# Three of the four weight sums of a seven-product matmul moved from VectorE to accumulating DMAs

## The chip, the core and the metric

The kernel runs on one core of one Trainium2 chip. The metric is the device time of one execution in microseconds (us). The kernel before takes 1199.08 us in the median of three runs (1198.47 to 1199.55).

## The reference, cut to what matters

The program is one layer of a decoder trunk for 512 tokens of width 1024, all in float32. What the change touches is the first mixer, retention with four heads. For each head h the layer projects the normed input u onto q and k (256 columns each), v (512 columns) and a gate g (512 columns), and then retains:

```
u = rmsnorm(h, g_pre_mix)
rq, rk, rv, rg, ... = split(u @ w_in)
yr = retention(rq, rk, rv, positions)          # scores, decay, scores @ v, chunk by chunk
yr = rmsnorm(yr) * silu(rg)
ya_branch = yr @ w_ret_out
```

Behind it come the dilated attention's output, two merge gates, `w_o`, an MLP with a squared ReLU (`w_up`, `w_down`), and a last gated projection. None of that is touched.

## The kernel before

**Splitting.** A float32 product is made of three TensorE passes in the fp32r type. Each operand is split into a high part (ScalarE writes the rounded copy, line 66) and a low part (VectorE subtracts it from the source, line 69): `split`, lines 71 to 73. The passes are high*high, high*low and low*high.

**Weight units.** Weights come in units of 256 rows by 512 columns, 512 KB, a raw tile of 128 partitions by 1024 elements. SyncE loads them in the order of the list `loads` (`load_next`, line 94). The list `plan` says how the raw tile of each unit is come by. `prep_next` (line 121) takes the next plan entry, makes a `w` tile of six in a ring and splits into it. It is called each time TensorE's program has used up one unit (line 744), so units are prepared some five ahead, and a split waits until the unit six back has been used.

**Seven products.** A head's v and g columns together are one matmul of 512 tokens by 1024 by 1024. It is done as a 2x2 block product with seven block products in place of eight. The order (`EARLY`, line 139) is 11, 1, 12, 2, 4, 7, 22; each product takes two weight units, k=0 and k=1. The weight blocks are quarters of `w_in`, written here by their indices: (0,0), (0,1), (1,0), (1,1). Four of the seven products need sums of quarters, per unit k:

- product 11 takes x = (0,0) as it is;
- product 1 takes x + y with y = (0,1);
- product 12 takes (1,0) as it is;
- product 2 takes x + y + z with z = (1,1);
- product 4 takes z as it is;
- product 7 takes y + z;
- product 22 takes x + y + z + (1,0), and (1,0) is loaded a second time for it.

The sums are made in place by VectorE (`add`, line 149, through `tt`, line 69): the rows `t<-t,t 128x1024`. So a head has 4 sums times 2 units, 8 of them, and 10 unit loads.

**A head on TensorE.** `head` (line 772) runs the q and k projection (line 256), the products 11 and 1 (line 740), the scores (line 812), the products 12, 2, 4 and 7, the retention of the first two token blocks (line 827), the product 22 and the retention of the other two. Products 11 and 12 share a pair of PSUM banks, 1 and 4 another, and 2, 7 and 22 a third. The scores go to banks of the same pool as the third pair, which has four: product 2 can begin only after VectorE has multiplied scores with the decay (`s<-b,dec`) and freed banks. The result of product 1 (`s<-a,s`, line 707) must be read before product 4 adds to its banks.

**GpSimd.** In this stretch it does one thing, the power -0.5 for each retained token block (`rstd`, line 327, operation `st<-st,mhalf`). VectorE's gate multiply (line 833) waits for it, and TensorE later transposes the gate's result (line 849).

**The order of instructions** on each engine is set by a scheduler when the program is built. The order on TensorE is the program's; on the others it goes by priorities and the scheduler's own clock.

Of the kernel before, what the change touches and what calls it, by code (L numbers as in the profile page):

```python
# [14 lines left out]
OP = mybir.AluOpType  # L15
# [16 lines left out]
def hybrid_block(ctx, tc, a, out):  # L32
    nc = tc.nc
# [16 lines left out]
    def big(shape=(P, D), dtype=F32):  # L50
        return pt.tile(list(shape), dtype, name=nm("t"), tag="t")
# [13 lines left out]
    def act(o, i, f=AF.Copy, **kw):  # L65
        nc.scalar.activation(o, i, f, **kw)  # L66

    def tt(o, x, y, op):
        nc.vector.tensor_tensor(o, x, y, op=op)  # L69

    def split(hi, lo, src):
        act(hi, src)
        tt(lo, src, hi.bitcast(F32), OP.subtract)
# [16 lines left out]
    loads, plan = [], []  # L90
    raws, ready = [], []
    ptr = {"dma": 0, "prep": 0}

    def load_next():
        if ptr["dma"] < len(loads):
            r = big((P, 2, 512))
            load(r, loads[ptr["dma"]])
            raws.append(r)
            ptr["dma"] += 1

    def pop():
        if not raws:
            load_next()
        return raws.pop(0)

    def new_w():
        return pw.tile([P, 2, 2, 512], F32R, name=nm("w"), tag="w")
# [3 lines left out]
    def divide(w, r, gain):  # L111
        if gain is None:
            split(w[:, 0], w[:, 1], r)
            return
        n, k0 = gain
        for k in range(2):
            g = cols[:, n, k0 + k:k0 + k + 1]
            act(w[:, 0, k], r[:, k], AF.Copy, scale=g)
            stt(w[:, 1, k], r[:, k], g, w[:, 0, k].bitcast(F32), OP.mult, OP.subtract)

    def prep_next():
        if ptr["prep"] == len(plan):
            return
        ptr["prep"] += 1
        r = plan[ptr["prep"] - 1]()
        w = new_w()
        divide(w, r, row_gain.get(ptr["prep"] - 1))
        ready.append(w)
        while len(raws) < N_RAW - 1 and ptr["dma"] < len(loads):
            load_next()  # L130

    def add_units(w, n, gain=None):
        for kk in range(w.shape[1]):
            loads.append(w[n, kk])
            if gain is not None:
                row_gain[len(plan)] = (gain, 2 * kk)
            plan.append(pop)

    EARLY, LATE = ("11", 1, "12", 2, 4, 7, "22"), ("11", 1, 2, 4, 7, "12", "22")

    def add_quartet(quarter, order, between=(), nk=2, gaps=(1, 1, 1, 1, 1, 1, 2)):
        x, y, z, v = {}, {}, {}, {}
        again = order is EARLY

        def keep(d, k):
            d[k] = pop()
            return d[k]

        def add(a, b):
            tt(a, a, b, OP.add)  # L150
            return a

        make = {
            "11": ((0, 0), lambda k: keep(x, k)),
            1: ((0, 1), lambda k: add(x[k], keep(y, k))),
            2: ((1, 1), lambda k: add(x[k], keep(z, k))),
            4: (None, lambda k: z[k]),
            7: (None, lambda k: add(y[k], z[k])),
            "12": ((1, 0), lambda k: pop() if again else keep(v, k)),
            "22": ((1, 0) if again else None, lambda k: add(x[k], pop() if again else v[k])),  # L160
        }
        for name in order:
            src, f = make[name]
            for k in range(nk):
                if src is not None:
                    loads.append(quarter(*src, k))
                plan.append(lambda f=f, k=k: f(k))
            m = gaps[order.index(name)]
            for src, f, gain in between[:m]:
                loads.append(src)  # L170
                row_gain[len(plan)] = gain
                plan.append(f)
            between = between[m:]

    w_in, w_ro, w_do = a["w_in"], a["w_ret_out"], a["w_dil_out"]
# [5 lines left out]
    for h in range(H):  # L181
        add_units(w_in, 3 * h)
        if not h:
            for n in range(2):
                add_units(w_do, n)
        add_quartet(lambda kh, nh, k, h=h: w_in[3 * h + 2 - nh, 2 * kh + k], EARLY)
    for h in range(H):
        for n in range(2):
            add_units(w_ro[h], n)
# [13 lines left out]
    for c in range(NC):  # L203
        ups = [(a["w_up"][2 * c + 2 + j, k], pop, (3, 2 * k)) for j in range(2 if c + 1 < NC else 1) for k in range(4)]
        add_quartet(lambda kh, nh, k, c=c: a["w_down"][2 * c + kh, nh, k], EARLY, ups, 2, gaps_of(c))
    ups = [(a["w_up"][NFC - 1, k], pop, (3, 2 * k)) for k in range(4)]
    add_quartet(lambda kh, nh, k: a["w_down"][NFC - 2, nh, kh], EARLY, ups, 1, SOME)
    for n in range(2):
        add_units(a["w_down"][NFC - 1], n)
# [51 lines left out]
    def gemm(nu, xT, evac, wstat=False, k_outer=False):  # L261
        us = take(nu)
        if k_outer:
            banks = [abank() for _ in range(4)]
            for k in range(2 * nu):
                for t in range(4):
                    acc_tile(banks[t], us, xT, t, wstat, None, [k])
                    if k == 2 * nu - 1:
                        if t == 3:
                            prep_next()  # L270
                        evac(t, banks[t])
                if k % 2 and k < 2 * nu - 1:
                    prep_next()
            return
        for t in range(4):
            ps = abank()
            acc_tile(ps, us, xT, t, wstat, prep_next if t == 3 else None)
            evac(t, ps)
# [14 lines left out]
    for i in range(4):  # L293
        x = big((P, 2, 512))
        r = big((P, 2, 512))
# [19 lines left out]
    def stt(o, x, s, y, op0=OP.mult, op1=OP.mult):  # L315
        return nc.vector.scalar_tensor_tensor(o, x, s, y, op0=op0, op1=op1)  # L316

    def rstd(parts, n, out=None):
        s = parts[0]
        for p2 in parts[1:]:  # L320
            s2 = stat()
            tt(s2, s, p2, OP.add)
            s = s2
        v = stat()
        nc.vector.tensor_scalar(v, s, 1.0 / n, EPS, op0=OP.mult, op1=OP.add)
        r = stat() if out is None else out
        nc.gpsimd.tensor_tensor(r, v, mhalf[:, :1], op=OP.pow)
        return r
# [21 lines left out]
    for i in range(4):  # L350
        w = new_w()
        r = pop()
        for j in range(2):
            f = 2 * i + j
            g = cols[:, 0, f:f + 1]
# [4 lines left out]
        ptr["prep"] += 1  # L360
        load_next()
    prep_next()
    uT = feed(u)

    rs0 = const.tile([P, NT], F32, name="rs0")
    for t in range(NT):
        x = xr[t]
# [564 lines left out]
    for t in range(NT):  # L932
        x = big()
# [82 lines left out]
    def part(t, n):  # L1016
        return facc[t][:, halves[n]]
# [66 lines left out]
    f = fs[0][0]  # L1084
# [11 lines left out]
    for t in range(NT):  # L1096
        parts = []
        for n in range(2):
# [4 lines left out]
            f = part(t, n)  # L1103
# [3 lines left out]
        with tc.high_priority():  # L1107
            r = rstd(parts, D)
# [34 lines left out]
    for t in range(NT):  # L1143
# [8 lines left out]
        with tc.high_priority():  # L1152
            r = rstd(parts[t], D)
# [80 lines left out]
```

## Time and profile before

| | before |
|---|---|
| median of three runs | 1199.08 us |
| the profiled execution | 1198.07 us |
| its span, first to last instruction | 1196.3 us |
| TensorE busy | 1183.7 us (99%) |
| VectorE busy | 813.7 us (68%) |
| ScalarE busy | 588.5 us (49%) |
| GpSimd busy | 65.3 us (5%) |
| moved by DMA | 158.35 MB |

The span begins with the first instruction and ends with the last; the profiled execution's own time holds 1.8 us more around it. Busy is the time in which an engine had an instruction running. The profile calls TensorE PE (its weight loads PEld), VectorE DVE, ScalarE ACT, GpSimd POOL and SyncE SP. L69 is line 69 of the kernel; many operations are issued by a helper and share its line, so the tile names tell them apart: `w` is a split weight unit, `t` a raw or other big tile, `s` a half tile, `a` and `b` PSUM banks, `dec` the decay.

### The profile page before, as it was taken

How to read it: one execution, taken by the hardware profiler on the slowest of the kernel's cores; microseconds unless marked ns; L12 is line 12 of the kernel's file. 1: busy time of each engine (PE TensorE's matmuls, PEld its weight loads, DVE VectorE, ACT ScalarE, POOL GpSimd, SP SyncE). 2: the span in 40 equal slices, each digit the busy share in tenths (PEclk: the TensorE clock that was granted, in tenths of full speed). 3: DMA queues.
4: the chain of work that ended last, by engine and by line, in shares of the span. 5: the costliest groups of instructions: out<-in, count | busy, mean ns of one | idle time of the engine just before them, and what ended most of it. 6: DMA issues, size and time to landing. Idle time of an engine off the chain costs nothing.

```text
span 1196.3 us, 15173 instructions
## 1 busy us (share of the span) xinstructions
PE 1183.7 (99%) x5634; PEld 985.7 (82%) x5634; DVE 813.7 (68%) x1243; ACT 588.5 (49%) x1031; POOL 65.3 (5%) x112
## 2 busy tenths in 40 slices
PE   9999999999999999999999999999999999999996
PEld 7888888888888888888888888888888888888885
DVE  6753653664748995959678457663575775988885
ACT  7335524537545553535445622365553654544562
POOL 1002101000000010010100020020000000000210
PEclk9999999999999999999999999999999999999999
DMA  9431141432422542442336563735241251335401
GB/s 345 152 111 58 59 154 36 132 122 95 158 98 80 202 158 98 133 153 89 110 106 211 171 216 111 269 110 233 71 160 59 98 193 36 111 134 207 171 13 71
DMA packets 53178, 158.35 MB, mean 132 GB/s; under 512 B 8816, under 2 KB 9072, under 8 KB 53104
## 3 DMA queue, kind: packets, MB, share of 16 engines
q1 hardware_dynamic: 39408, 131.29, 31.7%
q10 hardware_dynamic: 9600, 14.54, 3.7%
q0 software_dynamic: 4096, 11.55, 2.7%
q8 instruction: 44, 0.72, 0.3%
q14 instruction: 30, 0.25, 0.1%
HBM read 138.96 MB, written 14.68 MB: 128 GB/s over the span
## 4 chain that ended last, share of the span: by engine, by line
PE 97%; ACT 1%; DVE 1%; DMA 1%; SPq 0%; issue 0%; ACTq 0%; DVEq 0%; POOLq 0%
PE a L256 53%; PE b L740 17%; PE a L1063 11%; PE a L740 7%; PE b L827 2%; PE b L531 2%; PE b L812 1%; PE b L495 1%; PE b L520 1%; ACT t L66 1%; PE b L339 1%; PE b L849 1%; DMA t<-in_w_in_dram 1%; DVE t L316 0%; DVE t L504 0%; PE b L623 0%
## 5 line engine op out<-in xcount | busy, mean ns | idle before, releaser
L256 PE MATMUL a<-u,w 128*128 128x512 f32 x1536 | 358.7, 392 | 1.2 <-ACT t L66 0.7
L256 PEld LDWEIGHTS a<-u,w 128*128 128x128 f32 x1536 | 285.7, 188 | 61.5 <-issue 1.0
L66 ACT ACTIVATE w<-t 128x1024 fp32r<-128x1024 f32 (+1 forms) x211 | 217.7, 1042 | 209.4 <-PE a L256 71.6
L69 DVE TENSOR_TENSOR w<-t,w 128x1024 fp32r<-128x1024 f32 (+1 forms) x211 | 251.4, 1200 | 95.1 <-ACT w L66 93.4
L69 DVE TENSOR_TENSOR t<-t,t 128x1024 f32<-128x1024 f32 (+4 forms) x193 | 196.6, 1043 | 32.5 <-ACT t L66 18.1
L740 PE MATMUL b<-w,t 128*128 128x512 f32 x780 | 182.7, 390 | 0.0
L740 PEld LDWEIGHTS b<-w,t 128*128 128x128 f32 x780 | 146.1, 188 | 31.2 <-ACT t L66 0.7
L1063 PE MATMUL a<-u,w 128*128 128x512 f32 x576 | 134.8, 389 | 0.0
L1063 PEld LDWEIGHTS a<-u,w 128*128 128x128 f32 x576 | 108.1, 188 | 22.5
L256 PE MATMUL a<-w,u 128*128 128x512 f32 (+1 forms) x504 | 113.2, 383 | 0.2 <-DVE w L69 0.2
L256 PE MATMUL a<-t,w 128*128 128x512 f32 x480 | 109.7, 390 | 0.0
L256 PEld LDWEIGHTS a<-w,u 128*128 128x128 f32 x504 | 91.3, 189 | 18.8 <-DVE w L69 0.5
L256 PEld LDWEIGHTS a<-t,w 128*128 128x128 f32 x480 | 89.9, 188 | 18.6
L316 DVE SCALAR_TENSOR_TENSOR w<-t,cols,w 128x512 fp32r<-128x512 f32 x80 | 57.5, 747 | 45.4 <-ACT w L66 45.3
L69 DVE TENSOR_TENSOR t<-a,t 128x512 f32<-128x512 f32 x64 | 50.3, 788 | 48.0 <-ACT t L66 34.3
L256 PE MATMUL a<-w,t 128*128 128x512 f32 x336 | 78.3, 392 | 0.0
L256 PEld LDWEIGHTS a<-w,t 128*128 128x128 f32 x336 | 62.4, 188 | 13.2 <-DVE t L69 0.3
L66 ACT ACTIVATE w<-t,cols 128x512 fp32r<-128x512 f32 x80 | 53.9, 716 | 38.4 <-PE a L1063 27.2
L66 ACT ACTIVATE t<-t 128x512 fp32r<-128x512 f32 (+1 forms) x62 | 46.3, 768 | 29.6 <-DVE t L69 28.7
L66 ACT ACTIVATE t<-s 128x256 f32<-128x256 f32 (+3 forms) x98 | 42.3, 476 | 26.5 <-DVE s L69 25.6
L69 DVE TENSOR_TENSOR s<-a,t 128x512 f32<-128x512 f32 x40 | 26.0, 686 | 41.3 <-PE a L256 30.7
L66 ACT ACTIVATE t<-t,st 128x128 f32<-128x128 f32 (+1 forms) x96 | 39.7, 416 | 26.8 <-DVE st L507 26.8
(120 smaller groups left out, 1028.8 us busy)
## 6 DMA issues: line engine op xcount, KB each, us to landing
t<-in_w_in_dram SPq DMA_DIRECT2D x104, 512.0 KB
t<-in_w_down_dram SPq DMA_DIRECT2D x39, 512.0 KB
t<-in_w_up_dram SPq DMA_DIRECT2D x32, 512.0 KB
t<-in_w_ret_out_dram SPq DMA_DIRECT2D x16, 512.0 KB
t<-in_x_dram SPq DMA_DIRECT2D x8, 512.0 KB
yrd<-s ACTq DMA_DIRECT2D x16, 256.0 KB
t<-yrd SPq DMA_DIRECT2D x16, 256.0 KB
t<-in_w_o_dram SPq DMA_DIRECT2D x8, 512.0 KB
```

Source lines behind the costliest of these rows:

```text
L66: nc.scalar.activation(o, i, f, **kw)
L69: nc.vector.tensor_tensor(o, x, y, op=op)
L256: nc.tensor.matmul(ps, l, r, start=(k == 0 and q == 0), stop=(k == n - 1 and q == 2))
L316: return nc.vector.scalar_tensor_tensor(o, x, s, y, op0=op0, op1=op1)
L339: nc.tensor.transpose(b[:, f * P:(f + 1) * P], src[:, f * P:(f + 1) * P], ident)
L495: nc.tensor.matmul(sb[hh][:, q * w:(q + 1) * w], at(qT, p0 + q)[rows, t * P:(t + 1) * P], at(kT, p0 + q)[rows, k0:k0 + w], start=True, sto ...
L520: nc.tensor.transpose(tb[:, c * P - h0:(c + 1) * P - h0], sm[:, i, j * P:(j + 1) * P], ident)
L531: nc.tensor.matmul(pv[:, s * HD:(s + 1) * HD], got["t"][:, c * P:(c + 1) * P], at(v, t - nb + 1 + j)[:, s * HD:(s + 1) * HD], start=(j == ...
L740: nc.tensor.matmul(ps[t], f(k, i, t), w[:, j, k2], start=(first and k == 0 and n == 0), stop=(k == 2 * nk - 1 and n == 2), skip_group_chec ...
L812: nc.tensor.matmul(b[:, :w], kT[d][:, i1, j * P:(j + 1) * P], qT[d][:, i2, j * P:], start=(n == 0), stop=(n == 5))
L827: nc.tensor.matmul(b, sc[j][:, i1, c:c + P], vh[j][:, i2, :], start=(n == 0), stop=(n == last))
L1063: nc.tensor.matmul(state["ps"][t], w[:, i, k2, t * P:(t + 1) * P], vT[:, x, k], start=(k == 0 and n == 0), stop=(k == 7 and n == 2))
```

## The change

In the heads' seven-product form (and not in the MLP's) the sums for the products 2, 7 and 22 are no longer made by VectorE. `add_quartet` gets a flag, set in the heads. With it, a DMA issued by GpSimd reads a quarter from DRAM and adds it onto the raw tile where that lies (`pour`, with `accum_op=OP.add`). After the split of product 1's unit k, two such DMAs add (1,1) onto x and onto y; after the split of product 2's unit k, one adds (1,0) onto x. Products 2, 7 and 22 then split x and y as they find them. Product 4's (1,1) becomes a load of its own, the loads for 2 and 22 go. The first sum, x + y for product 1, stays with VectorE.

```diff
--- before.py
+++ after.py
@@ -122,9 +122,13 @@
         if ptr["prep"] == len(plan):
             return
         ptr["prep"] += 1
-        r = plan[ptr["prep"] - 1]()
+        f = plan[ptr["prep"] - 1]
+        f, g = f if isinstance(f, tuple) else (f, None)
+        r = f()
         w = new_w()
         divide(w, r, row_gain.get(ptr["prep"] - 1))
+        if g:
+            g()
         ready.append(w)
         while len(raws) < N_RAW - 1 and ptr["dma"] < len(loads):
             load_next()
@@ -138,7 +142,7 @@
 
     EARLY, LATE = ("11", 1, "12", 2, 4, 7, "22"), ("11", 1, 2, 4, 7, "12", "22")
 
-    def add_quartet(quarter, order, between=(), nk=2, gaps=(1, 1, 1, 1, 1, 1, 2)):
+    def add_quartet(quarter, order, between=(), nk=2, gaps=(1, 1, 1, 1, 1, 1, 2), by_dma=False):
         x, y, z, v = {}, {}, {}, {}
         again = order is EARLY
 
@@ -159,12 +163,26 @@
             "12": ((1, 0), lambda k: pop() if again else keep(v, k)),
             "22": ((1, 0) if again else None, lambda k: add(x[k], pop() if again else v[k])),
         }
+
+        def pour(d, k, src):
+            nc.gpsimd.dma_start(d[k], quarter(*src, k), accum_op=OP.add)
+
+        behind = {}
+        if by_dma:
+            make.update({
+                2: (None, lambda k: x[k]),
+                4: ((1, 1), lambda k: pop()),
+                7: (None, lambda k: y[k]),
+                "12": ((1, 0), lambda k: pop()),
+                "22": (None, lambda k: x[k]),
+            })
+            behind = {1: lambda k: (pour(x, k, (1, 1)), pour(y, k, (1, 1))), 2: lambda k: pour(x, k, (1, 0))}
         for name in order:
             src, f = make[name]
             for k in range(nk):
                 if src is not None:
                     loads.append(quarter(*src, k))
-                plan.append(lambda f=f, k=k: f(k))
+                plan.append((lambda f=f, k=k: f(k), behind.get(name) and (lambda g=behind[name], k=k: g(k))))
             m = gaps[order.index(name)]
             for src, f, gain in between[:m]:
                 loads.append(src)
@@ -183,7 +201,7 @@
         if not h:
             for n in range(2):
                 add_units(w_do, n)
-        add_quartet(lambda kh, nh, k, h=h: w_in[3 * h + 2 - nh, 2 * kh + k], EARLY)
+        add_quartet(lambda kh, nh, k, h=h: w_in[3 * h + 2 - nh, 2 * kh + k], EARLY, by_dma=True)
     for h in range(H):
         for n in range(2):
             add_units(w_ro[h], n)
```

Per head there are 6 accumulating DMAs of 512 KB, 8 loads in place of 10, and 2 sums on VectorE in place of 8; over four heads that is 24 DMAs more, 8 loads fewer and 24 VectorE instructions fewer. The order on TensorE is the same row for row.

On VectorE, in the third head (h = 2), before the change. `t612` and `t614` are x for k=0 and k=1, `t628` is y for k=0, `t665` and `t667` are z; `w678` and `w684` are the split units of product 2, `w686` that of product 4; `s687` and `s688` are the results of product 1; `s690` is the first score times decay:

```order
615 L69 TENSOR_TENSOR w678_4527<-t612_4176,w678_4527 128x1024
616 L69 TENSOR_TENSOR t614_4193<-t614_4193,t667_4477 128x1024
617 L69 TENSOR_TENSOR s687_4571<-a682_4536,s680_4532 128x512
618 L69 TENSOR_TENSOR t628_4245<-t628_4245,t665_4466 128x1024
619 L69 TENSOR_TENSOR s688_4573<-a683_4537,s681_4534 128x512
620 L69 TENSOR_TENSOR w684_4551<-t614_4193,w684_4551 128x1024
621 L69 TENSOR_TENSOR w686_4568<-t665_4466,w686_4568 128x1024
622 L69 TENSOR_TENSOR s690_4582<-b689_4575,dec534_3727 128x512
```

After the change, the same place. `t608` and `t610` are x for k=0 and k=1, `w674` and `w679` product 2's units, `w680` and `w696` product 4's, `s682` and `s683` the results of product 1, `s685` the first score times decay:

```order
602 L69 TENSOR_TENSOR w674_4522<-t608_4168,w674_4522 128x1024
603 L69 TENSOR_TENSOR w679_4544<-t610_4185,w679_4544 128x1024
604 L69 TENSOR_TENSOR w680_4560<-t661_4462,w680_4560 128x1024
605 L69 TENSOR_TENSOR s682_4565<-a677_4530,s675_4526 128x512
606 L69 TENSOR_TENSOR s683_4567<-a678_4531,s676_4528 128x512
607 L69 TENSOR_TENSOR w696_4629<-t663_4473,w696_4629 128x1024
608 L69 TENSOR_TENSOR s685_4576<-b684_4569,dec532_3723 128x512
```

The sums are gone, and the two splits of product 2, which now wait for accumulating DMAs, stand next to each other ahead of product 1's results and of the scores.

On GpSimd, before, from the second head's powers to the third's:

```order
39 L327 TENSOR_TENSOR st621_4212<-st620_4210,mhalf_132 128x1
40 L327 TENSOR_TENSOR st626_4227<-st625_4225,mhalf_132 128x1
41 L327 TENSOR_TENSOR st635_4283<-st634_4281,mhalf_132 128x1
42 L327 TENSOR_TENSOR st640_4304<-st639_4302,mhalf_132 128x1
43 L327 TENSOR_TENSOR st728_4792<-st727_4790,mhalf_132 128x1
```

After, the same stretch. `t624` and `t626` are the third head's y for k=0 and k=1:

```order
51 L345 TENSOR_TENSOR st617_4204<-st616_4202,mhalf_132 128x1
52 L345 TENSOR_TENSOR st622_4219<-st621_4217,mhalf_132 128x1
53 L168 DMA t624_4237<-in_w_in_dram 128x1024
54 L345 TENSOR_TENSOR st631_4275<-st630_4273,mhalf_132 128x1
55 L168 DMA t626_4254<-in_w_in_dram 128x1024
56 L345 TENSOR_TENSOR st636_4296<-st635_4294,mhalf_132 128x1
57 L168 DMA t608_4168<-in_w_in_dram 128x1024
58 L168 DMA t610_4185<-in_w_in_dram 128x1024
59 L168 DMA t608_4168<-in_w_in_dram 128x1024
60 L168 DMA t610_4185<-in_w_in_dram 128x1024
61 L345 TENSOR_TENSOR st722_4780<-st721_4778,mhalf_132 128x1
```

The DMAs onto y for the next head stand between the powers of the third and fourth token block of the head before; the four onto x stand together behind them.

## Rows read from the trace of the kernel before

**Rows 1.** From the page's parts 1 and 2: the span, busy time of TensorE and VectorE (us, share, instructions), and the clock that TensorE was granted in 40 slices, in tenths.

```profile
span 1196.3 us, 15173 instructions
...
PE 1183.7 (99%) x5634; PEld 985.7 (82%) x5634; DVE 813.7 (68%) x1243; ACT 588.5 (49%) x1031; POOL 65.3 (5%) x112
...
PEclk9999999999999999999999999999999999999999
```

**Rows 2.** Who waited for whom, for TensorE in the whole program: who waited, for whom, us in total, times, longest.

```profile
PE b L290 <- DVE s L287: 1.5, 1, 1.5
PE a L256 <- ACT t L66: 0.7, 1, 0.7
PE a L256 <- ACT w L66: 0.5, 1, 0.5
PE a L256 <- DVE w L69: 0.2, 1, 0.2
```

**Rows 3.** Busy time of each engine in two stretches, the heads and what follows them up to the last part: us of the stretch, then PE, PEld, DVE, ACT, POOL (and instructions), granted clock, DMA share, GB/s.

```profile
340.00:665.00 325.00, 325.00 (x1505) 271.66 (x1504) 253.39 (x332) 160.86 (x228) 11.93 (x15) 1.00 0.38 128
665.00:1100.00 435.00, 435.00 (x1942) 359.90 (x1942) 292.86 (x364) 215.13 (x338) 17.03 (x30) 1.00 0.41 143
```

**Rows 4.** Groups of VectorE's instructions in the heads, 340 to 665 us, shapes apart: count, busy us, mean ns of one, idle time before them and what ended it. The first are the low halves of the units' splits, the second the weight sums.

```profile
L69 DVE TENSOR_TENSOR w<-t,w 128x1024 fp32r<-128x1024 f32 x80 | 97.0, 1220 | 17.2 <-ACT w L66 16.0
L69 DVE TENSOR_TENSOR t<-t,t 128x1024 f32<-128x1024 f32 x32 | 38.6, 1219 | 1.2 <-DMA t<-in_w_in_dram 1.2
```

**Rows 5.** TensorE in order of time in the third head: start us, us, operation, count. The rows are products 11 and 1, the scores, product 2, product 7 (12 and 4 lie between).

```profile
541.40 5.60 PE L740 MATMUL a<-w,u 128*128 128x512 f32 x24
546.84 5.60 PE L740 MATMUL a<-w,t 128*128 128x512 f32 x24
552.28 3.92 PE L812 MATMUL b<-t,t 128*128 128x512 f32 x24
...
561.53 5.60 PE L740 MATMUL b<-w,t 128*128 128x512 f32 x24
...
572.41 5.60 PE L740 MATMUL b<-w,t 128*128 128x512 f32 x24
```

**Rows 6.** VectorE in order of time in the third head. The rows are: the splits of product 1 (k=0, 1); the sum for product 2, k=0; its split; the sum for k=1; product 1's result, first half; the sum for product 7, k=0; the splits of product 2, k=1, and of product 4, k=0; scores times decay, three of them.

```profile
538.61 2.59 DVE L69 TENSOR_TENSOR w<-t,w 128x1024 fp32r<-128x1024 f32 x2 [1.76 <-ACT w L66]
541.11 1.22 DVE L69 TENSOR_TENSOR t<-t,t 128x1024 f32<-128x1024 f32 x1
...
548.72 1.22 DVE L69 TENSOR_TENSOR w<-t,w 128x1024 fp32r<-128x1024 f32 x1
549.86 1.22 DVE L69 TENSOR_TENSOR t<-t,t 128x1024 f32<-128x1024 f32 x1
551.12 0.69 DVE L69 TENSOR_TENSOR s<-a,s 128x512 f32<-128x512 f32 x1
551.73 1.22 DVE L69 TENSOR_TENSOR t<-t,t 128x1024 f32<-128x1024 f32 x1
...
553.46 2.35 DVE L69 TENSOR_TENSOR w<-t,w 128x1024 fp32r<-128x1024 f32 x2
555.73 1.48 DVE L69 TENSOR_TENSOR s<-b,dec 128x512 f32<-128x512 f32 x3
```

**Rows 7.** ScalarE in order of time in the third head: the high half of one unit's split.

```profile
538.88 1.06 ACT L66 ACTIVATE w<-t 128x1024 fp32r<-128x1024 f32 x1 [0.30 <-PE a L256]
```

**Rows 8.** VectorE in order of time in the first head (h = 0): the split of product 1, k=1; the sum for product 2, k=0, with the wait ahead of it; scores times decay.

```profile
399.53 1.21 DVE L69 TENSOR_TENSOR w<-t,w 128x1024 fp32r<-128x1024 f32 x1
...
403.68 1.23 DVE L69 TENSOR_TENSOR t<-t,t 128x1024 f32<-128x1024 f32 x1 [1.20 <-DMA t<-in_w_in_dram]
...
412.38 1.48 DVE L69 TENSOR_TENSOR s<-b,dec 128x512 f32<-128x512 f32 x3
```

**Rows 9.** TensorE in order of time in the first head: the beginning of product 2.

```profile
417.05 1.29 PE L740 MATMUL b<-w,t 128*128 128x512 f32 x5
```

**Rows 10.** The DMA view: the queue of SyncE's loads (packets, MB, share of 16 engines' time), and of the DMAs issued by GpSimd those of 512 KB from DRAM and of 256 KB (count, KB each, us from issue to landing).

```profile
q1 hardware_dynamic: 39408, 131.29, 31.7%
...
t<-ybd POOLq DMA_DIRECT2D x8, 256.0 KB, 4.6
...
t<-h1d POOLq DMA_DIRECT2D x4, 512.0 KB, 5.1
```

**Rows 11.** GpSimd in order of time where it issues those four of 512 KB: start us, us.

```profile
1098.85 0.58 POOL L1093 DMA_DIRECT2D t<-h1d  x1 [295.24 <-DVE w L316]
1100.88 1.67 POOL L1093 DMA_DIRECT2D t<-h1d  x3 [1.45 <-DVE w L69]
```

**Rows 12.** GpSimd in order of time at the end of the second head: the powers for the third and the fourth token block.

```profile
517.39 1.46 POOL L327 TENSOR_TENSOR st<-st,mhalf 128x1 f32<-128x1 f32 x1 [5.59 <-DVE st L325]
519.84 0.55 POOL L327 TENSOR_TENSOR st<-st,mhalf 128x1 f32<-128x1 f32 x1 [0.99 <-DVE st L325]
```

**Rows 13.** VectorE in order of time there: the third head's sum x + y for k=1, and the gate of the fourth token block.

```profile
517.22 1.23 DVE L69 TENSOR_TENSOR t<-t,t 128x1024 f32<-128x1024 f32 x1
...
520.42 0.75 DVE L316 SCALAR_TENSOR_TENSOR s<-b,st,s 128x512 f32<-128x512 f32 x1 [0.73 <-POOL st L327]
```

**Rows 14.** TensorE in order of time there: the first transposes of gated blocks.

```profile
526.02 1.03 PE L849 MATMUL b<-ident,s 128*128 128x128 f32 x8
```

## The prediction

> **What bounds the kernel now.** I read the page first. TensorE is busy for 1183.7 of 1196.3 us at the full granted clock, VectorE for 813.7 [rows 1]: one engine is saturated and the change works on another. Busy can hide waits, so the next view is who waited for whom: in the whole program TensorE waited 1.5 us for VectorE's first memset and 1.4 us for all else, 0.7, 0.5 and 0.2 [rows 2]. The table by stretches says the same of the heads: TensorE is busy in all 325 of 325 us [rows 3]. Weight loads are a second witness, since each has its matmul: 271.66 us of 325 is 0.836, and 359.90 of 435 in the stretch behind is 0.827 [rows 3]. The heads are streamed at least as densely as the rest. Head by head, product follows product without a gap: 541.40, 546.84, then the scores at 552.28 [rows 5].
>
> VectorE is at 253.39 of 325 us in the heads, 78% [rows 3]. It is behind nobody: the time saved there is idle time on an engine that TensorE isn't waiting for.
>
> **The change, part by part.**
>
> *Sums taken off VectorE.* The group has 32 sums, of which 24 go: 24 x 1.219 = 29.3 us [rows 4]. VectorE's share falls to (253.4 - 29.3) / 325 = 69%. On the path of the end this is worth 0 us, since no wait of TensorE in the heads ends with it. The most that it could give is all of the 1.4 us of rows 2, though these waits lie on ScalarE for the larger part; I take 0.
>
> *Loads.* Eight loads on SyncE go, and product 4's load comes later in the program than product 2's did. In the first head the sum for product 2 waited 1.20 us for its load [rows 8]; that wait goes with the sum, and product 4's load has one product more time. TensorE wasn't behind it: 0 us.
>
> *Issue on GpSimd.* Issuing a 512 KB DMA holds GpSimd 0.58 us, or 1.67 / 3 = 0.56 [rows 11]. 24 of them are 14 us, on an engine that is busy for 11.93 of 325 us in the heads [rows 3]. Behind them in its queue are the powers of the third and fourth token block. The DMA onto y (k=0) may go when VectorE's x + y is done, which stands on VectorE ahead of the input of the power; the one for k=1 follows the sum at 517.22 [rows 13], after the power for the third block. The fourth block's power then begins at most one issue later. Its gate ended at 520.42 + 0.75 = 521.17 [rows 13], and TensorE transposes gated blocks first at 526.02 [rows 14]: a cover of 4.85 us for about 0.6. Cost 0.
>
> *The new wait.* The split of product 2 now waits for a DMA that could only start after product 1's split, where before it waited for a VectorE instruction of 1.22 us. Behind it on VectorE stand, in the order shown with the change, the other split of product 2, product 4's first, the two results of product 1, product 4's second split and the scores times decay; ScalarE holds the high halves of the same splits. TensorE waits for that: product 2 needs its two units and two banks that the scores give back. I work back from product 2's start at 561.53 [rows 5]. From the landing of the last DMA onto x, the chain is one high half, 1.06 [rows 7], three low halves, 3 x 1.22 [rows 4], two results of product 1, 2 x 0.69 [rows 6], and two scores at 1.48 / 3 = 0.49 each, say 1.24 since the first are the widest: 7.3 us. So it must land by 554.2. It is issued when the second split of product 1 ends, 538.61 + 2.59 = 541.20 [rows 6]. **Allowed from issue to landing: 13.0 us** in the third head, and the second and fourth are built alike. In the first head the second split ends earlier than that against its product 2: 399.53 + 1.21 = 400.74 [rows 8] to 417.05 [rows 9], with the chain 1.22 us shorter (product 4's second split stands behind the scores there), 6.1 us: landing by 410.9, **10.2 us allowed**.
>
> The other DMAs have more. Those onto y are issued near 518 and wanted by product 7 at 572.41 [rows 5]. The one that adds (1,0) onto x is issued when product 2's split ends, 549.9 [rows 6]. Its reader, product 22's split, stands on VectorE ahead of product 2's results, and product 7 in the same banks waits for these at 572.41. One high half, one low half and two results of 0.69 make 3.7 us, so it must land by 568.7: 18.8 us allowed. Product 1's result moves behind two or three splits, from 551.12 to about 554; product 4, at 561.53 + 5.44 = 566.97, is the one that waits for it.
>
> *How long an accumulating DMA takes.* The trace has none. The nearest row is a plain DMA of the same size, direction and issuing engine: 5.1 us from issue to landing, with 4.6 for half the bytes [rows 10]. That is the lower end. In the queue 131.29 MB took 31.7% of 1196.3 us, so 0.524 MB hold the DMA engines for 1.51 us [rows 10]. An add must also read the tile: one more such pass gives 5.1 + 1.5 = 6.6 us, which I take. I know no ceiling from the rows; as the upper end I use three times the plain row, 15.3 us. With 6.6 us, and 1.5 more where the second of the pair queues behind the first, 8.1 us stand against 13.0 and 6.6 against 10.2: cost 0. The engines' load is no obstacle either: 24 x 3.0 - 8 x 1.5 = 60 us over 325 lift their share from 0.38 [rows 3] to about 0.57.
>
> The Trainium skill's page "Collectives: The Full Stack", in Part 3 on the bandwidth ceiling, says that the add in a DMA engine is free in itself but reads two sources through one ring, so that reducing runs at about half the rate of copying. By that rule the landing would be near 6.6 us and at most 10.2, and the sum stays at 0; no run here shows an accumulating DMA.
>
> **The sum.** 0 - 0 + 0 + 0: the span stays 1196.3 us and the profiled execution's own time 1198.07. The median of the runs is 1199.08, 1.0 above that execution, and the forecast is stated against the median: **1199.0 us**. A difference within 0.2%, 2.4 us, is what a measurement of this kernel can't tell from none.
>
> **Rivals.**
>
> *A. Accumulating DMAs are slow, and the wait lands on TensorE.* At 15.3 us the second DMA onto x lands at 541.2 + 15.3 = 556.5 against 554.2, 2.3 us late in each of three heads, and in the first at 416.0 against 410.9, 5.1 late: 12.0 us, 1211 us. It decides from about 12.6 us on, where the first head alone loses 2.4.. For it: nothing in the trace prices the add. Against it: the plain row would have to grow 2.5-fold. It is the one slower case I take seriously.
>
> *B. GpSimd becomes the gate.* If an accumulating DMA held GpSimd for 5 us rather than 0.6, the two onto y would delay the fourth block's gate by 10 us against the cover of 4.85: 5 us in each of three heads, 1214 us. It decides from 2.4 us per issue on. For it: a power beside VectorE's 1.23 us sum took 1.46 us in place of 0.55 [rows 12, 13], so GpSimd does get held up. Against it: this is a delay of 0.9 us, and the sums that hold it up mostly go. The page "SBUF — State Buffer" of the Trainium skill, section "Who interferes with whom", states the same for VectorE instructions with two SBUF inputs: they hold the read port that GpSimd shares. The trace agrees with that rule (1.46 against 0.55). By it each power, and a DMA's issue if it reads there, waits for at most one VectorE instruction of 1.23 us, so two in a row stay under 4.85.
>
> *C. VectorE's relief does reach TensorE.* For it: VectorE is the second busiest engine in the heads. Against it: rows 2 leave 1.4 us at most for the whole program, 1197.7 us, and that would still count as no change. To gain more, the idle 1196.3 - 1183.7 = 12.6 us of TensorE would have to shrink, which lie before and after the heads.
>
> *D. The DMAs don't take the sums' place,* as when the scheduler's order makes every accumulating DMA wait behind something late. In the order on GpSimd the DMAs onto x stand behind the powers, which end at 520.4, 20 us before the splits that they need: no loss, 1199 us, the same as the forecast.
>
> **How the numbers follow.** Forecast, with D: 0.75. A: 0.17. B: 0.04. C, strong enough to be measured: 0.04. So faster 0.04, same 0.75, slower 0.21. The likeliest case alone spans 1197.7 (all of rows 2) to 1201.5 (the first head a little late). To leave no more than 2 in 10 outside I carry the range into A up to 1207, about two thirds of its price at 15.3 us.
>
> **What would show it.** Right: TensorE's waits still sum to about 3 us, none of them in the heads; product 2 of the third head starts at 561.5; VectorE has 8 sums of 128x1024 there in place of 32; the accumulating DMAs land in 5 to 10 us. A: TensorE waits for VectorE or ScalarE ahead of product 2, in all heads, with VectorE idle on `t<-in_w_in_dram`. B: GpSimd's DMA rows take microseconds, and TensorE waits at line 849. The forecast is wrong if an accumulating DMA takes over 10 us from issue to landing, or if something that I hold to be hidden, on GpSimd or among the loads, sits on TensorE's path.

## The result, and the profile after

The changed kernel takes 1201.03 us (median of 13 runs, 1199.59 to 1201.95), the kernel before 1199.08 (13 runs, 1197.79 to 1200.00): a ratio of 1.0019, interval 1.0012 to 1.0026. The change makes the kernel 1.95 us slower. The forecast was 1199.0 us, no change; the measured time lies inside the stated range, but "no change" did not hold. One run below, of a_moved, took 2012.01 us at a mean granted clock of 0.555 and is slow; its ratio leaves it out, its median of 1198.47 doesn't (1198.38 without it).

The page of the changed kernel, its part 1, against [rows 1]:

```profile
span 1199.5 us, 15215 instructions
...
PE 1183.4 (99%) x5634; PEld 985.3 (82%) x5634; DVE 788.4 (66%) x1219; ACT 588.4 (49%) x1031; POOL 84.6 (7%) x136
```

VectorE has 24 instructions and 25 us less, GpSimd 24 instructions and 19 us more, and TensorE the same work. The span is 3.2 us longer. The table of who waited for whom, for TensorE, against [rows 2]:

```profile
PE b L308 <- DVE s L305: 1.5, 1, 1.5
PE a L274 <- ACT w L66: 1.4, 2, 0.9
PE a L274 <- ACT t L66: 1.4, 1, 1.4
PE a L274 <- DVE w L69: 0.2, 1, 0.2
```

The same four kinds of wait, 4.5 us in place of 2.9, and none of them is on the products of the heads (line 758); the 1.6 us more all lie in the first 60 us of the program, ahead of the heads. The table by stretches has the heads against [rows 3] (columns: stretch, its us, PE, PEld, DVE, ACT, POOL, granted clock, DMA share, GB/s):

```profile
340.00:665.00 325.00, 325.00 (x1505) 271.66 (x1504) 227.42 (x308) 161.09 (x228) 31.63 (x39) 1.00 0.55 153
```

TensorE is busy in all 325 us, with the same 271.66 us of weight loads as before. Nothing was lost there. So I looked at what comes after the last matmul, which no row ahead of the prediction shows. In the chain that ended last, the last piece on TensorE and the last piece of all, before:

```profile
1179.78 6.90 PE a L256 x53
...
1190.98 0.66 DVEq L1230
```

and after:

```profile
1179.88 8.03 PE a L274 x58
...
1192.22 0.66 DVEq L1248
```

TensorE ends at 1186.7 before and 1187.9 after (1.2 us later, of which more below), and both chains stop some 5 to 7 us ahead of the end of the span. What fills that gap is on a sequencer and isn't counted as busy: the instructions of the line on which the program ends. Of the kernel before (columns: engine, operation, count, ns min/median/max, first and last start):

```profile
L1230 POOLq DRAIN  x3: 40/98/5892, 1189.6 to 1196.0; - x3
L1230 SPq DRAIN  x3: 7/7/7, 1193.9 to 1195.8; - x3
```

and of the changed one:

```profile
L1248 POOLq DRAIN  x3: 46/97/7847, 1190.9 to 1199.2; - x3
L1248 SPq DRAIN  x3: 7/7/7, 1195.1 to 1199.0; - x3
```

GpSimd's first drain takes 5.89 us before, 7.85 after: **1.96 us more, the measured difference.** It starts at GpSimd's last power (1189.6; 1190.9) and ends at 1195.5 and 1198.7. SyncE, which waits there for the last stores to land, was ready at 1193.9 and at 1195.1 (the first start of its own drain), so in both kernels the end of the program waits for GpSimd: by 1.6 us before, by 3.6 after. From the end of the last matmul to the end of the span it is 9.63 us before, 11.59 after.

The other 1.2 us of the longer span come from elsewhere and differ from one execution to the next. The 111th matmul, in the loading of the first tiles, starts at 29.78 us in the one and 30.80 in the other; over the profiled executions of this study that start ranges from 29.46 to 31.95, in code that is the same in all of them. From there to the start of the last matmul it is 1156.60 us before, 1156.83 after, and 1156.47 to 1156.78 in the runs below other than a_twice. So I compare tails and medians below, not spans.

Where 24 DMAs more on GpSimd make its drain 1.96 us longer, that is 0.082 us for each. Before, GpSimd issues 64 DMAs, and 64 x 0.082 = 5.2 us of the 5.89; the power that it also waits for, 0.55 us, is most of the rest. Four theories go into the experiments: COUNT (the drain takes 0.082 us for every DMA that GpSimd has issued, whatever it moves), PACKETS (it goes by the packets in GpSimd's queue, the first number of its row `q0`: 4096 before and 7552 after), ADD (only accumulating DMAs lengthen the end) and HEADS (the loss is in the heads, and the drain beside the point). GpSimd's queue before (packets, MB, share of the time of 16 engines):

```profile
q0 software_dynamic: 4096, 11.55, 2.7%
```

### The profile page after: what moved, and what is told of

Same layout as the page of the kernel before. It is cut to its first block, busy times and chain, and to the rows that moved or that the text cites. A ratio compares the mean times of both kernels' runs of the same rounds, so it can differ in the third digit from the quotient of the medians.

```text
span 1199.5 us, 15215 instructions
## 1 busy us (share of the span) xinstructions
PE 1183.4 (99%) x5634; PEld 985.3 (82%) x5634; DVE 788.4 (66%) x1219; ACT 588.4 (49%) x1031; POOL 84.6 (7%) x136
## 3 DMA queue, kind: packets, MB, share of 16 engines
q0 software_dynamic: 7552, 24.14, 8.6%
## 4 chain that ended last, share of the span: by engine, by line
PE 96%; ACT 2%; DMA 1%; DVE 1%; issue 0%; SPq 0%; ACTq 0%; DVEq 0%; POOLq 0%
PE a L274 53%; PE b L758 16%; PE a L1081 10%; PE a L758 7%; PE b L845 2%; PE b L549 2%; PE b L830 1%; PE b L513 1%; PE b L538 1%; ACT t L66 1%; PE b L357 1%; PE b L867 1%; DMA t<-in_w_in_dram 1%; ACT w L66 0%; ACT s L66 0%
## 5 line engine op out<-in xcount | busy, mean ns | idle before, releaser
L69 DVE TENSOR_TENSOR t<-t,t 128x512 fp32r<-128x512 f32 (+4 forms) x169 | 167.8, 1017 | 30.3 <-ACT t L66 18.2
```

## The experiments

| kernel | DMAs of GpSimd | its drain at the end, us | last matmul to end, us | time, us | ratio to before |
|---|---|---|---|---|---|
| before | 64 | 5.89 | 9.63 | 1199.08 | |
| changed | 88 | 7.85 | 11.59 | 1201.03 | 1.0019 (1.0012 to 1.0026) |
| b_tiny24 | 88 | 7.85 | 11.59 | 1200.60 | 1.0013 (1.0004 to 1.0022) |
| b_wide24 | 88 | 7.85 | 11.59 | 1200.67 | 1.0018 (1.0009 to 1.0027) |
| b_tiny48 | 112 | 9.81 | 13.55 | 1202.56 | 1.0028 (1.0019 to 1.0038) |
| a_moved | 64 | 5.89 | 9.63 | 1198.47 | 0.9998 (0.9989 to 1.0007) |
| b_moved | 40 | 3.93 | 8.02 | 1197.05 | 0.9983 (0.9974 to 0.9992) |
| b_drain | 64 | 0.64 | 8.00 | 1197.49 | 0.9989 (0.9980 to 0.9997) |
| a_drain | 88 | 0.65 | 8.01 | 1197.06 | 0.9984 (0.9975 to 0.9993) |
| b_both | 40 | 0.64 | 8.01 | 1197.45 | 0.9991 (0.9982 to 1.0000) |
| b_nosum | 64 | 5.89 | 9.93 | 1198.87 | 1.0002 (0.9993 to 1.0011) |
| a_twice | 92 | 8.17 | 11.91 | 1208.83 | 1.0079 (1.0066 to 1.0093) |

Times are medians of 11 runs, of 13 in the first two rows, 9 of b_tiny48 and 4 of a_twice. Ratios, with their 95% intervals, are to runs of the kernel before made beside each (their medians lie between 1198.47 and 1199.08). b_ stands on the kernel before, a_ on the changed one. b_nosum leaves the sums out and a_twice adds one quarter twice, so neither computes the layer.

**b_tiny24: 24 tiny plain DMAs added to the kernel before,** in the MLP, where GpSimd has nothing else to do.

```diff
+    junk = const.tile([P, 192], F32, name="junk")
+    for i in range(24):
+        nc.gpsimd.dma_start(junk[:1, 8 * i:8 * i + 8], h1d[3][:1, 8 * i:8 * i + 8])
     facc = [big() for _ in range(NT)]
```

> The kernel before with 24 further plain DMAs on GpSimd's queue in the MLP, each of 32 bytes from one partition, with a result that nothing reads. Theory COUNT (the drain of GpSimd at the end of the program takes about 0.083 us for every DMA that GpSimd has issued: 5.32 us from its last power for 64 of them before, 7.27 for 88 after): the drain goes from 5.89 to about 7.85 us, the time up by 1.95 us, ratio 1.0016, and nothing moves ahead of the last matmul. Theory PACKETS (the drain grows with the packets of GpSimd's queue: 1.95 us for 3456 more): 24 more packets are worth 0.01 us, ratio 1.0000. Theory ADD (only accumulating DMAs lengthen the end): drain 5.89, ratio 1.0000. Theory HEADS (the 2 us of the changed kernel are lost in the heads, and the longer drain is a bystander): ratio 1.0000.

Its queue, and its lines at the end of the program:

```profile
q0 software_dynamic: 4864, 11.56, 2.8%
```

```profile
L1233 POOLq DRAIN  x3: 40/93/7854, 1189.6 to 1198.0; - x3
L1233 SPq DRAIN  x3: 7/7/7, 1193.9 to 1197.8; - x3
```

The whole loss of the change is there, without an accumulating DMA, without a byte worth speaking of, and with the heads as they were: the last matmul ends at 1186.69 (1186.66 before) and SyncE is ready at 1193.9 as before. ADD and HEADS fall. PACKETS falls too, though the packets were not as I had put them: each tiny DMA counts 32, so 768 more, which would be worth 0.43 us; the drain grew by 1.96.

**b_wide24: the same with 128 partitions each.**

```diff
+    junk = const.tile([P, 192], F32, name="junk")
+    for i in range(24):
+        nc.gpsimd.dma_start(junk[:128, 8 * i:8 * i + 8], h1d[3][:128, 8 * i:8 * i + 8])
```

> The kernel before with 24 further plain DMAs on GpSimd's queue in the MLP, each of 32 bytes from each of 128 partitions, with a result that nothing reads. COUNT: drain about 7.85 us, ratio 1.0016, the same as with one partition. PACKETS: at least 24 x 128 = 3072 more packets, so 1.7 us or more, drain 7.6 or more, ratio 1.0014 or more. ADD: drain 5.89, ratio 1.0000. HEADS: 1.0000. Only together with the one of one partition does it tell COUNT from PACKETS.

```profile
L1233 POOLq DRAIN  x3: 40/98/7854, 1190.4 to 1198.7; - x3
```

The drain is the same to the nanosecond. As a test of PACKETS this run fails: its queue has 4864 packets too, not 3072 more, so that it differs from b_tiny24 in bytes alone. What separates packets from count is the next pair.

**b_tiny48 and a_moved: 48 tiny DMAs on the kernel before, of 16 bytes each; and the changed kernel with 24 of its plain DMAs on SyncE's queue.** The edit of a_moved:

```diff
-            yb, z0 = ([at(x, i) for i in range(KT)] for x in (fetch(ybd, nc.gpsimd.dma_start), fetch(z0d, nc.gpsimd.dma_start)))
+            yb, z0 = ([at(x, i) for i in range(KT)] for x in (fetch(ybd), fetch(z0d)))
...
-            nc.gpsimd.dma_start(at(e[n], t), ed[n][t])
+            nc.sync.dma_start(at(e[n], t), ed[n][t])
```

> The kernel before with 48 further DMAs on GpSimd's queue, of 16 bytes each. COUNT as a straight line: 112 DMAs, drain 5.89 + 48 x 0.0818 = 9.82 us, time up by 3.9 us, ratio 1.0033. If the drain has a step (so many DMAs of one batch) in place of a slope: 7.85 as with 24, or a jump to another value.

> The changed kernel with 24 other DMAs (the 16 loads of ybd and z0d, the 8 of ed) taken from GpSimd to SyncE's queue, so that GpSimd issues 64 again, 24 of them accumulating. COUNT: drain 5.89 us, time that of the kernel before, 1199.1, ratio 1.0000 (if the loads behind the moved ones on SyncE are not late). PACKETS: the same, since the moved ones had as many packets as the accumulating ones. ADD: drain still 7.85, 1201.0, ratio 1.0016. HEADS: 1201.0, ratio 1.0016, with a drain of 5.89.

GpSimd's queue and drain in b_tiny48:

```profile
q0 software_dynamic: 5632, 11.56, 2.8%
```

```profile
L1233 POOLq DRAIN  x3: 40/93/9812, 1190.9 to 1201.2; - x3
```

and in a_moved:

```profile
q0 software_dynamic: 5632, 17.85, 7.0%
```

```profile
L1248 POOLq DRAIN  x3: 46/98/5889, 1190.0 to 1196.4; - x3
L1248 SPq DRAIN  x3: 7/7/7, 1194.2 to 1196.2; - x3
```

Both queues have 5632 packets, and a_moved more bytes; the drains are 9.81 and 5.89 us. With 112 DMAs and 64, 24 of these accumulating, they lie on COUNT's line: the slope from 40 to 112 DMAs is (9.812 - 3.927) / 72 = 0.0817 us, and no point is off it by more than 0.01. In a_moved the time is back at that of the kernel before. So the accumulating DMAs themselves cost nothing that these runs can tell in the heads; their number on GpSimd costs, at the end.

**b_drain and a_drain: one more drain on GpSimd, where it is idle for 21 us.** The list keeps GpSimd's powers, so that the drain can be put behind the last one of the MLP.

```diff
+    pows = []
...
-        nc.gpsimd.tensor_tensor(r, v, mhalf[:, :1], op=OP.pow)
+        pows.append(nc.gpsimd.tensor_tensor(r, v, mhalf[:, :1], op=OP.pow))
...
+    with tc.issue_after(pows[-1].ins):
+        nc.gpsimd.drain()
     e = {n: pair_tiles() for n in range(2)}
```

> The kernel before with one more drain on GpSimd, behind the last power of the MLP's residual, where GpSimd then has 21 us without work (1152.5 to 1173.5). COUNT, with the further claim that what the drain does for a DMA is done once: the early drain takes some 5.3 us where nobody waits, the last one under 0.5 us, the end is then set by SyncE, which has seen the last store land at 1193.9 (span about 1194.7 in place of 1196.3): -1.6 us, ratio 0.9987. COUNT without that claim (each drain walks over all DMAs so far): the early one 5.3, the last one 5.9 again, ratio 1.0000. If the drain at the end is a fixed cost of ending a program: the early one short, the last 5.9, ratio 1.0000.

> The changed kernel with one more drain on GpSimd behind the last power of the MLP's residual, as in b_drain. COUNT, with the work done once: the early drain takes about 8.3 us (6.34 us for 64 DMAs in b_drain, and 24 x 0.083), the last one 0.6, the end is set by SyncE's wait for the last store: 1201.0 - 1.96 - 1.63 = 1197.4 us, ratio to the kernel before 0.9986, the same as b_drain. HEADS (part of the 2 us lost ahead of the last matmul): slower than b_drain by that part, up to 2 us, ratio 0.9987 to 1.0003.

The early drain of b_drain, and its lines at the end:

```profile
L1115 POOLq DRAIN  x1: 6337/6337/6337, 1153.8 to 1153.8; - x1
```

```profile
L1234 POOLq DRAIN  x3: 34/97/643, 1191.9 to 1196.7; - x3
L1234 SPq DRAIN  x3: 7/7/7, 1196.2 to 1196.5; - x3
```

The early drain of a_drain, and its lines at the end:

```profile
L1133 POOLq DRAIN  x1: 8301/8301/8301, 1153.1 to 1153.1; - x1
```

```profile
L1252 POOLq DRAIN  x3: 34/98/645, 1191.3 to 1196.1; - x3
L1252 SPq DRAIN  x3: 7/7/7, 1195.5 to 1195.8; - x3
```

The early drains differ by 8.30 - 6.34 = 1.96 us, again 24 x 0.082 (each also waits for a power of 1.0 us), and nobody waits for them. At the end 0.64 us are left, little more than the last power. SyncE comes last now, and the time from the last matmul to the end is 8.0 us in both kernels: 1.6 less than before, 3.6 less than in the changed one. That settles the claim that the work for a DMA is done once. With the early drain the changed kernel beats both kernels (1197.06 us), but b_drain, without the change, has the same tail and an overlapping interval: the gain is the drain's, not the change's.

b_drain's profiled span is 0.7 us longer than that of the kernel before although its median is shorter. What is late is the loading of the first tiles. The stretch from 9 to 14 us, before:

```profile
9.00:14.00 5.00, 4.78 (x21) 3.71 (x22) 3.89 (x7) 4.08 (x7) 0.00 (x0) 1.00 0.98 358
```

in b_drain, and the first matmul that starts in it, with the wait ahead:

```profile
9.00:14.00 5.00, 3.99 (x12) 2.98 (x13) 3.54 (x6) 4.19 (x7) 0.00 (x0) 0.78 1.01 333
```

```profile
9.78 0.49 PE L256 MATMUL a<-w,u 128*128 128x512 f32 x1 [1.59 <-ACT w L66]
```

and in b_both (below), whose 111th matmul starts at 31.62 us, against 31.95 in b_drain:

```profile
9.00:14.00 5.00, 4.05 (x16) 3.11 (x17) 3.83 (x6) 4.48 (x7) 0.00 (x0) 1.00 0.94 318
```

In b_drain TensorE waited 1.59 us for a split and was then granted the lower of its two levels (0.50, that is 1.2 GHz) from 12 to 15 us, and from there to the last matmul the program is 2.2 us late. b_both was granted the full clock in that stretch, so the clock is a part of the lateness in one execution and not its cause in all. Why an execution gets this start or the other stays open; code that is the same in all of them gives either.

**b_moved and b_both: the same 24 plain DMAs moved to SyncE in the kernel before; and that with the early drain.**

> The kernel before with 24 DMAs (16 loads of ybd and z0d, 8 of ed) taken from GpSimd to SyncE's queue: 40 are left. COUNT: drain 5.89 - 24 x 0.0818 = 3.93 us, over at about 1193.55, just ahead of SyncE at 1193.92, so that SyncE sets the end: span 1194.7, -1.6 us, ratio 0.9987, the same as b_drain by another road. If the loads behind the moved ones come late: TensorE waits near 715 or 1130 us, ratio 1.000 or more.

> The kernel before with both remedies: the 24 plain DMAs on SyncE's queue (b_moved) and the early drain (b_drain). SYNCE SETS THE END once GpSimd's last drain is shorter than SyncE's wait for the last store: the two remedies don't add, the early drain takes about 4.4 us, the last 0.6, the ratio is 0.9985 as with each alone. ADDITIVE (the drain itself costs, wherever it lies): below 0.998.

The end of b_moved:

```profile
L1230 POOLq DRAIN  x3: 46/97/3927, 1189.4 to 1194.2; - x3
L1230 SPq DRAIN  x3: 7/7/7, 1193.7 to 1194.0; - x3
```

40 DMAs, 3.93 us as expected, over at 1193.4, and SyncE ready at 1193.75: SyncE sets the end by 0.4 us. The early drain of b_both, and its last:

```profile
L1115 POOLq DRAIN  x1: 4384/4384/4384, 1153.9 to 1153.9; - x1
```

```profile
L1234 POOLq DRAIN  x3: 34/98/636, 1191.5 to 1196.3; - x3
```

The early one takes 4.38 us and the last 0.64, and the tail is 8.01 like that of each remedy alone: they don't add, since what is left is the wait for the last store. The moved loads made nothing late.

**b_nosum: the relief of VectorE alone.** The raw tiles go into the splits unsummed; the loads stay.

```diff
+        if not sums:
+            make[2] = ((1, 1), lambda k: (keep(z, k), x[k])[1])
+            make[7] = (None, lambda k: y[k])
+            make["22"] = ((1, 0), lambda k: (pop(), x[k])[1])
```

> The kernel before with the 24 sums left out of the heads and nothing in their place (the raw tiles go into the splits unsummed; all loads stay). It has the relief of VectorE without the accumulating DMAs. The prediction's step (relief worth 0, TensorE waits for nobody in the heads): ratio 1.0000, TensorE's busy share of the heads unchanged, VectorE 29.3 us less. RELIEF COUNTS (the sums do hold TensorE up somewhere, and the pours took that gain back): faster by more than 1 us, ratio 0.999 or less.

```profile
340.00:665.00 325.00, 325.00 (x1504) 271.64 (x1504) 228.20 (x308) 161.82 (x228) 11.05 (x15) 1.00 0.37 129
```

VectorE is relieved by 25 us in the heads (the sums last 29.3, but neighbours overlap in the records, as in [rows 6], where the split ends at 541.20 and the sum begins at 541.11, so a sum fills less busy time than it lasts), TensorE's 325 us stay, and the time stays. Its tail is 0.3 us longer with the same drain, because the last power comes 3.3 us behind the last matmul in place of 3.0. So the sums were worth nothing beyond the 0.1% that the interval leaves, and the accumulating DMAs didn't hide a gain.

**a_twice: how much later could the sums have been?** The last accumulating DMA ahead of product 2 is issued twice.

```diff
-            behind = {1: lambda k: (pour(x, k, (1, 1)), pour(y, k, (1, 1))), 2: lambda k: pour(x, k, (1, 0))}
+            behind = {1: lambda k: (pour(x, k, (1, 1)), *[pour(x, k, (1, 1)) for _ in range(k)], pour(y, k, (1, 1))), 2: lambda k: pour(x, k, (1, 0))}
```

> The changed kernel with the second accumulating DMA of each head's pair onto x (k=1) issued twice, so that product 2's and product 22's sums are wrong by w(1,1) in that half; the second of the two waits for the first to land, so the sum is there about 14.1 us after the issue in place of 7.0. It prices rival A and tests the prediction's two limits. LIMITS RIGHT (landing by 13.0 us after the first issue in heads two to four, 10.2 us in the first): in the third head landed at 542.53 + 14.1 = 556.6 against 554.2 + 1.0 (this trace runs 1.0 later) = 555.2, 1.4 late in three heads; in the first at 402.33 + 14.1 = 416.4 against 411.9, 4.5 late; 8.7 us of waits of TensorE ahead of product 2, and 4 more DMAs in the drain, 0.3: 1201.0 + 9.0 = 1210 us, ratio 1.0092. LIMITS TOO TIGHT (TensorE has more cover than I counted): 1201.4, ratio 1.0019, no waits in the heads. LIMITS TOO LOOSE (the real cover ended near 7 us): about 7 us in each head, 1229 us, ratio 1.025.

TensorE's waits in the whole program, the first row:

```profile
PE b L758 <- DVE s L69: 5.8, 1, 5.8
```

Its first head in order of time, on TensorE (start us, us, ..., and the wait ahead in brackets) and on ScalarE:

```profile
417.93 1.52 PE L758 MATMUL b<-w,t 128*128 128x512 f32 x6
425.27 5.82 PE L758 MATMUL b<-w,t 128*128 128x512 f32 x18 [5.83 <-DVE s L69]
```

```profile
420.70 2.00 ACT L66 ACTIVATE w<-t 128x1024 fp32r<-128x1024 f32 x2 [13.64 <-DMA t<-in_w_in_dram]
```

One wait, 5.83 us, in the first head; after it the granted clock is at the lower of its two levels (0.50, that is 1.2 GHz) to 428 us, 0.58 on average from 425 to 429, and from the 111th matmul to the last it takes 1164.24 us in place of 1156.83, 7.4 more, to which the drain of four more DMAs adds 0.3: 7.7 of the 7.8 measured. In the third head the second landing is there at 562.64, 12.7 us after the first issue, and TensorE doesn't wait. So the limit of 13.0 for heads two to four wasn't passed by this run (the second landing took 5.7 us, not 7.1), and the 10.2 for the first head was too tight: by this wait the split could have started at 420.70 - 5.83 = 414.9, 12.7 us after the issue at 402.16.

## Why the prediction was right and wrong

**Wrong: the cost of the DMAs on GpSimd.** The step is "Issue on GpSimd ... Cost 0", and with it the sum, "0 - 0 + 0 + 0: the span stays 1196.3 us". It priced what an issue delays in GpSimd's queue, the next power and the gate behind it, and that part held. It left out what each issue adds to GpSimd's drain at the end: 24 x 0.0817 = 1.96 us, uncovered, because GpSimd was already the engine that everything waited for there. The prediction says itself that TensorE's idle 12.6 us "lie before and after the heads", and has no term for the end of the program. The chain of work stops at 1191.6, 4.7 us ahead of the span's end, and I didn't ask what stands in that gap; the rows of the program's last line show it in the kernel before: 5.89 us, ending 1.6 us behind SyncE. That the 64 DMAs caused it can't be read from one kernel; that whatever lengthens that drain is paid in full can.

**Wrong by consequence: where the slower cases were looked for.** A (a slow add) and B (a GpSimd that is held) both put the loss in the heads. Both conditions failed: the median landing is 7.0 us against A's 12.6, and an issue 0.86 against B's 2.4. That the range holds 1201.03 all the same is luck: its upper side was put there for accumulating DMAs that come late, and none did.

**Right: the sums are worth nothing.** b_nosum shows it alone (1.0002, 0.9993 to 1.0011), a_moved together with the pours (0.9998). C falls. VectorE's share was to fall to 69% and is 227.42 / 325 = 70%.

**Right, with sizes a little off: the accumulating DMAs.** In the changed kernel, the queues, and the accumulating and the plain row of 512 KB:

```profile
q1 hardware_dynamic: 38256, 127.10, 30.5%
q0 software_dynamic: 7552, 24.14, 8.6%
...
t<-in_w_in_dram POOLq DMA_DIRECT2D x24, 512.0 KB, 7.0
t<-h1d POOLq DMA_DIRECT2D x4, 512.0 KB, 5.5
```

and their issue and landing by line:

```profile
L168 POOL DMA_DIRECT2D t<-in_w_in_dram x24: 842/855/922, 385.6 to 625.1; - x24
...
DMA to landing us min/median/max: 5.4/7.0/9.5
```

7.0 us against the 6.6 that I took, with 5.4 to 9.5 around it. In the queue GpSimd's DMAs took 8.6% of 1199.5 us in place of 2.7% of 1196.3 us: 70.9 us more for 24, 2.95 each against 3.0 estimated and 1.5 for a plain one. The Trainium skill's rule of half the rate (page "Collectives: The Full Stack", Part 3), which the page states for the reduce step of a ring of cores, agrees with this trace: 2.95 against 1.5. The DMA engines' share in the heads was to be 0.57 and is 0.55. An issue takes 0.86 us, half as much again as the plain one's 0.58 that I took; the cover of 4.85 us for it was not used up: in the third head's stretch the fourth block's gate ended at 522.28 and the transposes began at 527.06.

**Right, with one limit mis-sized: the new wait.** The third head's product 2, in order of time, and ScalarE's split that waits for the first head's second landing:

```profile
562.57 5.60 PE L758 MATMUL b<-w,t 128*128 128x512 f32 x24
```

```profile
411.68 2.96 ACT L66 ACTIVATE w<-t 128x1024 fp32r<-128x1024 f32 x3 [4.46 <-DMA t<-in_w_in_dram]
```

561.53 was forecast, and of the 1.04 us more the later start of this execution is 1.02; there is no wait ahead. In the first head the unit came 411.68 - 402.33 = 9.35 us after its issue, among the longest, and by my limit (410.9, and 1.0 for the later start) that left 0.2 us. By a_twice the limit lay 3 us further: TensorE starts product 2 and needs the bank that the late splits hold up only after six matmuls, where my chain had to be over when the product starts. The working erred on the safe side.

**The bound of 0.2%.** I put it as what a measurement can tell from no change. 13 runs of each kernel tell 0.07%, and the difference was 0.19%.

## What to carry to other kernels

In this kernel TensorE is saturated, and time saved on VectorE in the middle was worth nothing, while GpSimd's last instruction cost its full price. So read what stands between the last matmul and the end of the span, on the sequencers' rows of the program's last line, before calling an addition on any engine free. Each DMA issued by GpSimd put 0.082 us on that engine's drain here, so use another engine's queue where nothing needs GpSimd's, or let GpSimd drain once in a stretch where it is idle. Add a dummy of the suspected kind (b_tiny24) before believing a mechanism that only the change itself shows.

## What the runs showed of the hardware that I had not expected

- GpSimd's drain takes 0.0817 us for every DMA that the engine has issued since the last drain, from 40 to 112 of them, whether a DMA moves 16 bytes or 512 KB, copies or adds, and some 0.66 us besides, most of it the wait for a power; a drain in between resets it (0.64 us at the end). The Trainium skill's page "VectorE: DVE Perf Modes", section "The DRAIN you can't avoid", says that the drains put at a program's start and end take a constant 12 ns or so on all five engines. SyncE's 7 ns agree; GpSimd's 3.93 to 9.81 us don't, and the measurement decides. What the engine does in that time no record shows.
- A DMA of 32 bytes and one of 4 KB from 128 partitions on GpSimd's queue both count 32 packets (4864 - 4096 = 768 for 24).
- A wait of 5.8 us in the middle of the program cost TensorE 7.4 (a_twice): the clock granted behind it was 0.58 for 4 us, which by that share is 1.7 us more.
